# Sums of the norm for the seven products: from GpSimd and VectorE after one plain unit to VectorE alone after three

## The chip, the cores and the metric

The kernel runs on one core of a Trainium2 chip. The metric is the device time of one execution in microseconds, the median of several runs.

## What is computed

The reference is a two-layer backbone on 256 context and 512 latent tokens, 768 in all, of width 1024. Each layer has three mixers, a merge, and a gated MLP. The change touches the MLP of the first layer alone, the only one that runs over all 768 tokens:

```python
def conv_ffn(xn, w_up, conv_w, w_down):
    u = dwconv(xn @ w_up, conv_w)          # w_up is 1024 x 5632, conv of width 3 over positions
    a, gt = jnp.split(u, 2, axis=-1)
    return (a * jax.nn.silu(gt)) @ w_down  # w_down is 2816 x 1024
```

Here `xn` is the modulated norm of the residual stream.

## The kernel before

**Two parts of each number.** Each float32 operand of a product is split into a rounded high part and a low rest (`split`, line 220: a ScalarE copy makes the high part, a subtraction on VectorE the low one). A product is then three matmuls: high by high, high by low, low by high. The norm is held so too, as `n01xh` and `n01xl`, with eight k-blocks of 128 channels by 768 tokens.

**The MLP, `ffn` (line 1794).** The 22 column blocks of gates and of values run in pairs, `p0` = 0 and 2 inside groups `f0` = 0, 4, 8 and so on. For each pair first the gates (two blocks of 128 columns), then the values. One such pair of blocks is called a unit here: `f0g00` is the gates of pair 0, `f0a00` its values, `f0g02` and `f0a02` those of the second pair, `f0g40` the gates of the first pair of the next group. After `f0g40` stands the down projection `f0d0` of the group before it. A finished block goes through the convolution on VectorE (lines 1813 and 1815), the values through a product on GpSimd (line 1830), and then a split into `f0gh` and `f0gl` (lines 1831 and 1832).

**Two ways to compute a unit.** A plain unit (`gemm_fm`, line 247) takes each block with 8 k-blocks, three matmuls each, over 512 and then 256 tokens. A unit of seven products (`gemm7`, line 308) works on quarters, halves of k by halves of the tokens (384), and needs sums of quarters: four halves of weights made on GpSimd (`half`, lines 323 to 326) and four sums of the norm. It has seven groups of 12 matmuls on 384 tokens in place of eight. The groups and what they read of the sums, in the order of the code: `x1` (none), `x6` (sum 3), `x7` (sum 2), `x5` (sum 1), `x1` again (none), `x7` again (sum 4), `x5` again (none).

**The sums, `norm_sums` (line 622).** Four additions on GpSimd restore the quarters of the norm from its parts (line 632), four subtractions on VectorE make the sums (line 635), and four splits make their parts. Sum 2 is written over the quarter of the norm that no product of `gemm7` reads, so it has to wait for the plain units that read it. In the kernel before, `norm_sums` stands behind unit `f0a00`, and `f0g02` is the first unit of seven products.

**What sets the order.** Inside the MLP a scheduler orders each engine's instructions ahead of time by its own estimate of when each is ready, and among the ready by priority: program order, shifted by `high(offset)`. A negative offset puts work behind. The order on an engine is then fixed. Buffers of a tag share a number of slots: `q6` (line 156) holds the quarters, the sums and the `f0gh`, `f0gl` pairs, `s4` holds the fourth sum of weights. Weights come by DMA into four `wraw` slots and their parts into three `wh` and three `wl` slots. Between units, single products of the conditioning (`adp`, `adc`, lines 541 and 573) are put in.

Of the kernel before, what the change touches and what calls it, by code (L numbers as in the profile page):

```python
# [9 lines left out]
F32 = mybir.dt.float32  # L10
F32R = mybir.dt.float32r
I32 = mybir.dt.int32
AF = mybir.ActivationFunctionType
ALU = mybir.AluOpType
# [6 lines left out]
NT = SEQ + CTX  # L21
# [84 lines left out]
class Kernel:  # L106
# [113 lines left out]
    def split(self, h, l, x, eng=None):  # L220

        if eng is None:
            eng = self.nc.vector
        self.nc.scalar.copy(h, x)
        eng.tensor_tensor(out=l, in0=x, in1=h.bitcast(F32), op=ALU.subtract)  # L225
# [82 lines left out]
    def gemm7(self, src, c0, x, nt, done, nm):  # L308


        nc = self.nc
        n = nt // 2
        xh, xl, T = x
        r0, r1 = [self.wraw(src[:, c0 + 128 * b:c0 + 128 * b + 128], KD, 128, f"{nm}r{b}") for b in range(2)]
        s23 = self.pi.tile([128, KD, 128], F32, name=f"{nm}s23", tag="s23", bufs=2)
        s4 = self.pi.tile([128, 4, 128], F32, name=f"{nm}s4", tag="s4", bufs=2)
        lo, hi = slice(0, 4), slice(4, 8)

        def half(out, a, b, op):
            with self.high(self.prio):  # L320
                nc.gpsimd.tensor_tensor(out=out, in0=a, in1=b, op=op)

        half(s23[:, hi], r0[:, lo], r1[:, lo], ALU.subtract)
        half(r1[:, lo], r1[:, lo], r1[:, hi], ALU.add)
        half(s23[:, lo], r1[:, lo], r0[:, lo], ALU.subtract)
        half(s4, r0[:, hi], s23[:, lo], ALU.subtract)
        w0 = self.wsplit(r0, KD, 128, f"{nm}w0")
        w23 = self.wsplit(s23, KD, 128, f"{nm}w23")
        w1 = self.wsplit(r1, KD, 128, f"{nm}w1")
        w4 = self.wsplit(s4, 4, 128, f"{nm}w4", nc.gpsimd)  # L330

        def prod(ps, w, o, h, l, start, stop):

            mm = lambda a, b, **kw: nc.tensor.matmul(ps, a, b, skip_group_check=True, **kw)
            for k in range(4):
                mm(w[0][:, o + k, :], h(k), start=(start and k == 0), stop=False)
                mm(w[0][:, o + k, :], l(k), start=False, stop=False)
                mm(w[1][:, o + k, :], h(k), start=False, stop=(stop and k == 3))

        def of(k0, c):  # L340
            return [lambda k, v=v: v[:, k0 + k, c] for v in (xh, xl)]

        def oft(i):
            return [lambda k, v=v: v[:, k, :] for v in T[i]]
        t0, t1 = slice(0, n), slice(n, nt)
        x1, x7 = self.pl(f"{nm}x1")[:, 0:n], self.pl(f"{nm}x7")[:, 0:n]
        x6, x5 = self.pb(f"{nm}x6")[:, 0:n], self.pb(f"{nm}x5")[:, 0:n]
        c = [self.st(f"{nm}c{b}") for b in range(2)]
        u = self.st(f"{nm}u")
        p1, u2, u3 = u[:, 0:n], u[:, n:2 * n], c[1][:, 0:n]  # L350
        add = dict(op=ALU.add)
        prod(x1, w0, 0, *of(0, t0), True, True)
        nc.scalar.copy(p1, x1)
        prod(x6, w23, 0, *oft(3), True, True)
        nc.vector.tensor_tensor(out=u2, in0=x6, in1=p1, **add)
        prod(x7, w23, 4, *oft(2), True, True)
        nc.vector.tensor_tensor(out=u3, in0=x7, in1=u2, **add)
        prod(x5, w1, 0, *oft(1), True, True)
        nc.vector.tensor_tensor(out=c[1][:, t1], in0=x5, in1=u3, **add)
        prod(x1, w0, 4, *of(4, t0), False, True)  # L360
        nc.scalar.copy(c[0][:, t0], x1)
        prod(x7, w1, 4, *oft(4), False, True)
        nc.vector.tensor_tensor(out=c[1][:, t0], in0=x7, in1=u2, **add)
        prod(x5, w4, 0, *of(4, t1), False, True)
        nc.vector.tensor_tensor(out=c[0][:, t1], in0=x5, in1=u2, **add)
        for b in range(2):
            done(b, [(c[b][:, a:e], (a, e)) for a, e in ((0, SEQ), (SEQ, nt)) if e > a])
            self.ada_next()
# [253 lines left out]
    def norm_sums(self):  # L622


        nc, N = self.nc, self.N
        nm, n = N["nm"], N["nt"] // 2
        xh, xl = N["x"]
        q = lambda v, k, t: v[:, 4 * k:4 * k + 4, n * t:n * t + n]
        R = {}
        for k, t in ((0, 0), (0, 1), (1, 1), (1, 0)):  # L630
            R[k, t] = self.q6(f"{nm}R{k}{t}").rearrange("p (k t) -> p k t", k=4)
            nc.gpsimd.tensor_tensor(out=R[k, t], in0=q(xh, k, t).bitcast(F32), in1=q(xl, k, t).bitcast(F32), op=ALU.add)

        def sub(o, a, b):
            nc.vector.tensor_tensor(out=R[o], in0=R[a], in1=R[b], op=ALU.subtract)
        sub((0, 0), (0, 1), (0, 0))
        sub((0, 1), (1, 1), (0, 1))
        sub((1, 1), (1, 1), (0, 0))
        sub((1, 0), (1, 0), (1, 1))
        T = {}  # L640
        for i, o in ((3, (1, 1)), (1, (0, 0)), (4, (1, 0)), (2, (0, 1))):
            if i == 2:
                T[i] = q(xh, 0, 1), q(xl, 0, 1)
            else:
                T[i] = [self.q6(f"{nm}T{v}{i}", F32R).rearrange("p (k t) -> p k t", k=4) for v in "hl"]
            self.split(*T[i], R[o])
        return xh, xl, T

    def norm_sq(self, j, a, b, eng=None):
        nc, N = self.nc, self.N  # L650
# [1143 lines left out]
    def ffn(self, l, xs, nt):  # L1794
        nc = self.nc
        nm = f"f{l}"
# [4 lines left out]
        for f0 in range(0, NFF, FG):  # L1801
            fn = min(FG, NFF - f0)
            gh, gl = [], []
            for p0 in range(0, fn, 2):
                keep = {}

                def conv(ch, res, tag):
                    w = [self.V("fv", 132 * l + 44 * k + ch) for k in range(3)]
                    a = self.st(f"{nm}{tag}")
                    for ps, (s, e) in res:  # L1810
                        n = e - s
                        nc.scalar.activation(a[:, s:e], ps, AF.Copy, scale=w[1])
                        nc.vector.scalar_tensor_tensor(out=a[:, s + 1:e], in0=ps[:, 0:n - 1], scalar=w[0],
                                                       in1=a[:, s + 1:e], op0=ALU.mult, op1=ALU.add)
                        nc.vector.scalar_tensor_tensor(out=a[:, s:e - 1], in0=ps[:, 1:n], scalar=w[2],  # L1815
                                                       in1=a[:, s:e - 1], op0=ALU.mult, op1=ALU.add)
                    return a

                def done_g(b, ps):
                    a = conv(NFF + f0 + p0 + b, ps, f"g{f0}{p0}{b}")  # L1820
                    nc.scalar.activation(a[:, :nt], a[:, :nt], AF.Silu)  # L1821
                    keep[b] = a

                def done_a(b, ps):
                    a = conv(f0 + p0 + b, ps, f"a{f0}{p0}{b}")
                    if b == 0:
                        gh.extend(self.pairs(f"{nm}gh{f0}{p0}", 1, F32R))
                        gl.extend(self.pairs(f"{nm}gl{f0}{p0}", 1, F32R))
                    h = gh[-1][:, b, :nt]
                    nc.gpsimd.tensor_tensor(out=a[:, :nt], in0=a[:, :nt], in1=keep[b][:, :nt], op=ALU.mult)  # L1830
                    nc.scalar.copy(h, a[:, :nt])  # L1831
                    nc.vector.tensor_tensor(out=gl[-1][:, b, :nt], in0=a[:, :nt], in1=h.bitcast(F32), op=ALU.subtract)  # L1832

                if f0 + p0 == 0:
                    self.gemm_first(KD, xs, done_g, f"{nm}g{f0}{p0}")
                    x7 = None
                elif x7:
                    self.gemm7(U, D_FF + 128 * (f0 + p0), x7, nt, done_g, f"{nm}g{f0}{p0}")
                else:
                    self.gemm_fm(U, D_FF + 128 * (f0 + p0), 256, KD, xs, done_g, f"{nm}g{f0}{p0}")  # L1840
                if down and f0 + FG < NFF:
                    self.gemm_fm(*down)
                    down = None
                if x7:
                    self.gemm7(U, 128 * (f0 + p0), x7, nt, done_a, f"{nm}a{f0}{p0}")
                else:
                    self.gemm_fm(U, 128 * (f0 + p0), 256, KD, xs, done_a, f"{nm}a{f0}{p0}")
                    if f0 + p0 == 0 and nt == NT:
                        x7 = self.norm_sums()
            segs = [((a, b), Blocks(gh, a, b), Blocks(gl, a, b)) for a, b in segb]  # L1850

            def done_d(j, res):
# [8 lines left out]
        last = l == DEPTH - 1  # L1861
# [64 lines left out]
    def body(self):  # L1926
        nc, tc = self.nc, self.tc
# [4 lines left out]
        for l in range(DEPTH):  # L1932
            nt = NT if l < DEPTH - 1 else SEQ
# [8 lines left out]
            with tc.tile_pool(name=f"t{l + 1}", bufs=1, reuse_waits="tile") as self.ph:  # L1942
# [7 lines left out]
                else:  # L1950
                    self.ada_fill(2)
                self.spare = nt < NT
                with self.inner(f"u{l}", 10):
                    xs = self.ffn(l, xs, nt)
                self.dump_h(f"hf{l}", nt)
                if l + 1 < DEPTH:
# [81 lines left out]
```

## Time and profile before

| what | value |
|---|---|
| median of 3 runs | 2674.77 us (2668.91 to 2679.19) |
| the profiled execution | 2679.46 us, its span 2677.7 us |
| TensorE busy, share of the span | 97% |
| VectorE, ScalarE, GpSimd | 63%, 39%, 17% |
| TensorE's granted clock, mean | 0.987 of full |

The span is the time from the first to the last instruction. A matmul's duration holds its passage through the array, so the pace of a run of matmuls is read from the distance of their starts. DVE is VectorE, ACT is ScalarE, POOL is GpSimd, PE is TensorE, SP is the engine that issues the DMAs.

### The profile page before, as it was taken

How to read it: one execution, taken by the hardware profiler on the slowest of the kernel's cores; microseconds unless marked ns; L12 is line 12 of the kernel's file. 1: busy time of each engine (PE TensorE's matmuls, PEld its weight loads, DVE VectorE, ACT ScalarE, POOL GpSimd, SP SyncE). 2: the span in 40 equal slices, each digit the busy share in tenths (PEclk: the TensorE clock that was granted, in tenths of full speed). 3: DMA queues.
4: the chain of work that ended last, by engine and by line, in shares of the span. 5: the costliest groups of instructions: out<-in, count | busy, mean ns of one | idle time of the engine just before them, and what ended most of it. 6: DMA issues, size and time to landing. Idle time of an engine off the chain costs nothing.

```text
span 2677.7 us, 44644 instructions
## 1 busy us (share of the span) xinstructions
PE 2584.4 (97%) x17161; PEld 2234.9 (83%) x17161; DVE 1699.3 (63%) x3605; ACT 1047.1 (39%) x2313; POOL 463.1 (17%) x362
## 2 busy tenths in 40 slices
PE   7999999999999997999999999999999999999999
PEld 5987988888888886899999988888877878888887
DVE  6666566746534658676786777856676646655555
ACT  5433355333432234343443454344633333433332
POOL 1010000001110426154445320000000203100000
PEclk9999999999999998999999999999999999999999
DMA  8364343546746322322212243522367675333332
GB/s 284 94 178 134 90 121 88 151 137 195 214 160 230 120 87 87 107 83 79 71 54 81 87 141 102 154 71 77 114 193 219 184 249 150 91 94 95 95 103 75
DMA packets 485223, 344.19 MB, mean 129 GB/s; under 512 B 48168, under 2 KB 450322, under 8 KB 484242
## 3 DMA queue, kind: packets, MB, share of 16 engines
q1 hardware_dynamic: 484721, 338.19, 42.6%
q8 instruction: 135, 2.21, 0.3%
q10 hardware_dynamic: 288, 3.15, 0.3%
q14 instruction: 79, 0.64, 0.1%
HBM read 285.23 MB, written 56.03 MB: 127 GB/s over the span
## 4 chain that ended last, share of the span: by engine, by line
PE 75%; DVE 10%; DMA 9%; issue 2%; ACT 1%; POOL 1%; SPq 1%; DVEq 0%; POOLq 0%; ACTq 0%
PE mg04p L265 1%; PE mg04p L266 1%; PE mg04p L264 1%; PE y0p L265 1%; PE y0p L264 1%; PE y0p L266 1%; PE adp L541 1%; PE mg14p L264 1%; PE mg14p L265 1%; PE mg14p L266 1%; PE y1p L264 1%; DMA m1mb<-g1rd 1%; PE y0op L264 1%; PE y0op L266 1%; PE y0op L265 1%
## 5 line engine op out<-in xcount | busy, mean ns | idle before, releaser
L1830 POOL TENSOR_TENSOR f1a<-f1a,f1g 128x512 f32<-128x512 f32 x22 | 28.5, 1295 | 311.8 <-DVE f1a L1815 292.3
L541 PE MATMUL adp<-ad,s 128*32 128x256 f32 x640 | 55.7, 405 | 6.5 <-DMA ad<-ada_w 5.6
L1830 POOL TENSOR_TENSOR f0a<-f0a,f0g 128x768 f32<-128x768 f32 x22 | 51.9, 2360 | 57.8 <-DVE f0a L1815 53.4
L1752 POOL TENSOR_TENSOR y0a<-y0a,y0g 128x768 f32<-128x768 f32 x16 | 33.2, 2079 | 118.1 <-DVE y0g L1749 115.8
L1107 POOL TENSOR_TENSOR m0qz<-m0qz,m0e 64x512 f32<-64x512 f32 x12 | 15.5, 1295 | 165.5 <-DVE mg04s5l L225 68.7
L541 PEld LDWEIGHTS adp<-ad,s 128*32 128x32 f32 x640 | 18.5, 112 | 26.3 <-issue 14.2
L1832 DVE TENSOR_TENSOR f0gl<-f0a,f0gh 128x768 fp32r<-128x768 f32 x22 | 31.0, 1411 | 8.5 <-ACT f0gh L1831 8.5
L1752 POOL TENSOR_TENSOR y1a<-y1a,y1g 128x512 f32<-128x512 f32 x16 | 24.2, 1513 | 57.8 <-DVE y1g L1749 56.6
L544 ACT COPY adr<-adp 128x256 f32<-128x256 f32 x40 | 14.8, 370 | 44.0 <-PE adp L541 42.8
L1831 ACT CAST f0gh<-f0a 128x768 fp32r<-128x768 f32 x22 | 18.4, 838 | 33.5 <-POOL f0a L1830 33.5
L1013 ACT ACTIVATE mg0t<-mg04p 128x512 f32<-128x512 f32 (+1 forms) x40 | 19.5, 486 | 25.2 <-PE mg04p L266 20.7
L1107 POOL TENSOR_TENSOR m1qz<-m1qz,m1e 64x512 f32<-64x512 f32 x8 | 11.2, 1406 | 102.9 <-DMA m1mb<-g1rd 45.7
L1821 ACT ACTIVATE f0g<-f0g 128x768 f32<-128x768 f32 x22 | 18.5, 846 | 22.8 <-DVE f0g L1815 22.8
L1749 DVE SCALAR_TENSOR_TENSOR y0g<-y0g,y0p 128x512 f32<-128x512 f32 (+1 forms) x32 | 17.3, 549 | 15.8 <-PE y0p L266 14.0
L1821 ACT ACTIVATE f1g<-f1g 128x512 f32<-128x512 f32 x22 | 13.9, 630 | 32.5 <-DVE f1g L1815 32.5
L1096 DVE SCALAR_TENSOR_TENSOR m0mb<-m0mb,g0a,cst 128x128 f32<-128x128 f32 x48 | 16.6, 404 | 15.3 <-DMA m0mb<-g0rd 14.3
L1773 DVE SCALAR_TENSOR_TENSOR hr<-y0op,y0gh,hr 128x512 f32<-128x512 f32 (+1 forms) x16 | 9.9, 617 | 25.8 <-PE y0op L266 25.8
L1169 POOL TENSOR_TENSOR rt<-rc,rw 128x256 f32<-128x256 f32 x4 | 3.0, 745 | 115.7 <-PE b0pk L1239 54.8
L1832 DVE TENSOR_TENSOR f1gl<-f1a,f1gh 128x512 fp32r<-128x512 f32 x22 | 15.1, 685 | 10.9 <-ACT f1gh L1831 10.7
L1831 ACT CAST f1gh<-f1a 128x512 fp32r<-128x512 f32 x22 | 13.5, 616 | 16.6 <-POOL f1a L1830 16.6
L1729 DVE TENSOR_TENSOR y0l<-y0ld,y0h 128x768 fp32r<-128x768 f32 x12 | 12.8, 1091 | 11.3 <-ACT y0h L1728 11.3
L1098 ACT ACTIVATE m0mb<-m0mb 128x512 f32<-128x512 f32 x12 | 7.6, 631 | 30.1 <-DVE m0mb L1096 25.4
(4586 smaller groups left out, 10220.2 us busy)
## 6 DMA issues: line engine op xcount, KB each, us to landing
ad<-ada_w SPq DMA_DIRECT2D x96, 512.0 KB, 4.3
mg04r<-w_in SPq DMA_DIRECT2D x20, 512.0 KB, 5.1
mg14r<-w_in SPq DMA_DIRECT2D x20, 512.0 KB, 6.0
y0g<-mg SPq DMA_DIRECT2D x24, 384.0 KB, 4.4
mg<-mg0t SPq DMA_DIRECT2D x24, 256.0 KB, 3.1
y0r<-w_branch SPq DMA_DIRECT2D x12, 512.0 KB, 3.6
mg<-mg1t SPq DMA_DIRECT2D x24, 256.0 KB, 3.5
y1r<-w_branch SPq DMA_DIRECT2D x12, 512.0 KB, 3.9
```

The lines of the kernel that those rows point to most:

```text
L264: nc.tensor.matmul(o, hv[:, k, :], xh[:, k, :], start=(k == 0), stop=False)
L265: nc.tensor.matmul(o, hv[:, k, :], xl[:, k, :], start=False, stop=False)
L266: nc.tensor.matmul(o, lv[:, k, :], xh[:, k, :], start=False, stop=(k == nk - 1))
L541: nc.tensor.matmul(ps[32 * j:32 * j + 32, 0:256], self.s32[:, 2 * k:2 * k + 32], raw[:, j, :], start=(q == 0), stop=(q == 1), tile_positio ...
L1013: nc.scalar.activation(s, o, AF.Tanh, scale=0.5)
L1107: nc.gpsimd.tensor_tensor(out=qd[r, d], in0=qd[r, d], in1=e2[r], op=ALU.mult)
L1749: nc.vector.scalar_tensor_tensor(out=(a if i == BR[0] else gt)[:, s:e], in0=gt[:, s:e], scalar=1.0, in1=ps, op0=ALU.add, op1=ALU.mult)
L1752: nc.gpsimd.tensor_tensor(out=a[:, :nt], in0=a[:, :nt], in1=gt[:, :nt], op=ALU.add)
L1821: nc.scalar.activation(a[:, :nt], a[:, :nt], AF.Silu)
L1830: nc.gpsimd.tensor_tensor(out=a[:, :nt], in0=a[:, :nt], in1=keep[b][:, :nt], op=ALU.mult)
L1831: nc.scalar.copy(h, a[:, :nt])
L1832: nc.vector.tensor_tensor(out=gl[-1][:, b, :nt], in0=a[:, :nt], in1=h.bitcast(F32), op=ALU.subtract)
```

## The change

The sums are taken from the two parts by VectorE alone: for sums 1 and 2 three instructions each (subtract the high parts, subtract the low parts, add), for sums 3 and 4 two each, with a split behind each sum. The call moves from behind `f0a00` to between `f0g02` and `f0a02`, with priority 3000 behind. The second pair is now plain too, and `f0g40` is the first unit of seven products. The split of sum 2 is issued on its own behind `f0a02`, at the usual priority. The `q6` slots in the MLP go from 10 to 11, those of `s4` from 2 to 1.

```diff
-        s4 = self.pi.tile([128, 4, 128], F32, name=f"{nm}s4", tag="s4", bufs=2)
+        s4 = self.pi.tile([128, 4, 128], F32, name=f"{nm}s4", tag="s4", bufs=1)
...
-        R = {}
-        for k, t in ((0, 0), (0, 1), (1, 1), (1, 0)):
-            R[k, t] = self.q6(f"{nm}R{k}{t}").rearrange("p (k t) -> p k t", k=4)
-            nc.gpsimd.tensor_tensor(out=R[k, t], in0=q(xh, k, t).bitcast(F32), in1=q(xl, k, t).bitcast(F32), op=ALU.add)
...
+        def diff(i, j, k):
+
+            for o, v in zip(R, (xh, xl)):
+                op(o, q(v, *j).bitcast(F32), q(v, *k).bitcast(F32), ALU.subtract)
+            op(R[0], R[0], R[1], ALU.add)
+
+        def less(o, j, a):
+            op(o, q(xh, *j).bitcast(F32), a, ALU.subtract)
+            op(o, o, q(xl, *j).bitcast(F32), ALU.add)
...
+        diff(1, (0, 1), (0, 0))
+        split(1, R[0])
+        less(R[1], (1, 1), R[0])
+        split(3, R[1])
+        less(R[0], (1, 0), R[1])
+        split(4, R[0])
+        diff(2, (1, 1), (0, 1))
+        T[2] = q(xh, 0, 1), q(xl, 0, 1)
+
+        def last():
+            self.split(*T[2], R[0])
+        return (xh, xl, T), last
...
+                if f0 + p0 == 2 and nt == NT:
+                    with self.high(-3000):
+                        sums, last_sum = self.norm_sums()
                 if x7:
                     self.gemm7(U, 128 * (f0 + p0), x7, nt, done_a, f"{nm}a{f0}{p0}")
                 else:
                     self.gemm_fm(U, 128 * (f0 + p0), 256, KD, xs, done_a, f"{nm}a{f0}{p0}")
-                    if f0 + p0 == 0 and nt == NT:
-                        x7 = self.norm_sums()
+                    if f0 + p0 == 2 and nt == NT:
+                        x7 = sums
+                        last_sum()
...
-                with self.inner(f"u{l}", 10):
+                with self.inner(f"u{l}", 11):
```

## Rows read from the trace of the kernel before

**Rows 1.** The page: busy time by engine, and TensorE in 40 slices.
```profile
PE 2584.4 (97%) x17161; PEld 2234.9 (83%) x17161; DVE 1699.3 (63%) x3605; ACT 1047.1 (39%) x2313; POOL 463.1 (17%) x362
...
PE   7999999999999997999999999999999999999999
```
**Rows 2.** Stages: busy us (and instructions) of each engine, clock, DMA share, GB/s.
```profile
1040.10:1053.50 13.40, 2.87 (x19) 0.72 (x18) 11.46 (x6) 2.18 (x3) 13.40 (x4) 0.63 0.66 195
1053.50:1073.20 19.70, 12.00 (x38) 9.86 (x38) 19.70 (x10) 6.48 (x6) 19.70 (x9) 0.65 0.00 0
```
**Rows 3.** The chain that ended last, in order of time: start, us, what.
```profile
1033.40 8.58 POOL n01R L632 x2
...
1042.01 4.95 DVE n01R L635
...
1052.03 3.20 DVE n01R L635
```
**Rows 4.** TensorE in order of time: start, us, instruction, [idle before <-releaser].
```profile
1018.94 0.39 PE L264 MATMUL f0a00p<-n01xh,f0a00s0h 128*128 128x512 f32 x1
...
1024.54 0.39 PE L264 MATMUL f0a00p<-n01xh,f0a00s1h 128*128 128x512 f32 x1
...
1031.33 0.28 PE L264 MATMUL f0a00p<-n01xh,f0a00s1h 128*128 128x256 f32 x1
...
1034.15 0.34 PE L334 MATMUL f0g02x<-n01xh,f0g02w0h 128*128 128x384 f32 x1
...
1036.23 0.38 PE L573 MATMUL adc<-cst,adr 128*128 128x128 f32 x2
1036.55 1.07 PE L541 MATMUL adp<-ad,s 128*32 128x256 f32 x16
...
1094.89 0.34 PE L334 MATMUL f0g40x<-n01xh,f0g40w0h 128*128 128x384 f32 x1
```
**Rows 5.** VectorE in order of time: sums, splits and convolutions.
```profile
1020.25 1.22 DVE L225 TENSOR_TENSOR f0a00s1l<-f0a00r,f0a00s1h 128x1024 fp32r<-128x1024 f32 x1
...
1032.18 2.04 DVE L1832 TENSOR_TENSOR f0gl<-f0a,f0gh 128x768 fp32r<-128x768 f32 x1
1034.14 0.74 DVE L1813 SCALAR_TENSOR_TENSOR f0a<-f0a00p,vec,f0a 128x511 f32<-128x511 f32 x1
...
1038.59 0.47 DVE L1813 SCALAR_TENSOR_TENSOR f0a<-f0a00p,vec,f0a 128x255 f32<-128x255 f32 x1
...
1050.21 1.74 DVE L635 TENSOR_TENSOR n01R<-n01R,n01R 128x1536 f32<-128x1536 f32 x1
...
1060.67 2.84 DVE L225 TENSOR_TENSOR n01Tl<-n01R,n01Th 128x1536 fp32r<-128x1536 f32 x1
```
**Rows 6.** GpSimd in order of time: the additions, a product, the fourth weight sums.
```profile
1029.32 1.85 POOL L1830 TENSOR_TENSOR f0a<-f0a,f0g 128x768 f32<-128x768 f32 x1
...
1033.37 16.88 POOL L632 TENSOR_TENSOR n01R<-n01xh,n01xl 128x1536 f32<-128x1536 f32 x4
1050.21 3.41 POOL L1830 TENSOR_TENSOR f0a<-f0a,f0g 128x768 f32<-128x768 f32 x1
...
1161.76 1.31 POOL L225 TENSOR_TENSOR f0a40w4l<-f0a40s,f0a40w4h 128x512 fp32r<-128x512 f32 x1
...
1177.16 2.03 POOL L225 TENSOR_TENSOR f0g42w4l<-f0g42s,f0g42w4h 128x512 fp32r<-128x512 f32 x1
```
**Rows 7.** ScalarE: the copy of one sum, with its wait.
```profile
1055.27 1.47 ACT L224 CAST n01Th<-n01R 128x1536 fp32r<-128x1536 f32 x1 [1.81 <-DVE n01R L635]
```
**Rows 8.** Stages as in rows 2: one plain unit here, then plain gates earlier.
```profile
1015.00:1034.00 19.00, 19.00 (x124) 15.98 (x123) 11.40 (x15) 9.44 (x13) 8.51 (x6) 1.00 0.27 84
...
830.00:880.00 50.00, 50.00 (x290) 44.01 (x290) 28.46 (x37) 11.59 (x13) 8.47 (x5) 1.00 0.63 207
```
**Rows 9.** TensorE by line, 1034 to 1095 us: busy, mean ns, idle before.
```profile
L541 PE MATMUL adp<-ad,s 128*32 128x256 f32 x48 | 4.5, 469 | 5.6 <-DMA ad<-ada_w 5.6
...
L573 PE MATMUL adc<-cst,adr 128*128 128x128 f32 x6 | 1.4, 329 | 0.5 <-ACT adr L544 0.5
```

More of the change, by code (lines that the diff above doesn't have):

```diff
@@ L628, in norm_sums, with op, split @@
         q = lambda v, k, t: v[:, 4 * k:4 * k + 4, n * t:n * t + n]
-        R = {}
-        for k, t in ((0, 0), (0, 1), (1, 1), (1, 0)):
-            R[k, t] = self.q6(f"{nm}R{k}{t}").rearrange("p (k t) -> p k t", k=4)
-            nc.gpsimd.tensor_tensor(out=R[k, t], in0=q(xh, k, t).bitcast(F32), in1=q(xl, k, t).bitcast(F32), op=ALU.add)
[L634 to L639, printed above, removed]
-        T = {}
[L641 to L647, printed above, removed]
+        R = [self.q6(f"{nm}R{i}").rearrange("p (k t) -> p k t", k=4) for i in range(2)]
+        T = {}
+        def op(o, a, b, op):
+            nc.vector.tensor_tensor(out=o, in0=a, in1=b, op=op)
+        def diff(i, j, k):
[5 more added lines that the diff above has]
+            op(o, o, q(xl, *j).bitcast(F32), ALU.add)
+        def split(i, v):
+            T[i] = [self.q6(f"{nm}T{p}{i}", F32R).rearrange("p (k t) -> p k t", k=4) for p in "hl"]
+            self.split(*T[i], v)
+        diff(1, (0, 1), (0, 0))
[9 more added lines that the diff above has]
+        return (xh, xl, T), last
     def norm_sq(self, j, a, b, eng=None):
```

## The prediction

> **What bounds the kernel now.** I read the busy shares first: TensorE is busy for 97% of the span, and of the 40 slices only the first and the sixteenth fall below nine tenths [rows 1]. The sixteenth holds the start of the first layer's MLP, so I cut that into stages [rows 2]. From 1040.1 us, 6 us into the first unit of seven products, TensorE is busy for 2.87 of 13.40 us, and then for 12.00 of 19.70 us at a mean clock of 0.65, a mix of its two levels of 1.2 and 2.4 GHz, after an idle stretch. GpSimd is busy all the while, and VectorE nearly so. The chain of waits says why: it runs through the additions on GpSimd into the subtractions on VectorE, and these into the splits [rows 3]. TensorE waits for the sums of the norm.
>
> **How much is lost there.** The first matmul of `f0g40` starts at 1094.89 us, so 60.74 us go by from the first one of `f0g02` [rows 4]. The work in them: one group of twelve matmuls on 384 tokens takes 2.08 us (1034.15 to 1036.23), so two units of seven groups take 29.1 us [rows 4]. Beside them ran 48 small products of the conditioning and six transposes [rows 9]; 16 of the first took 1.07 us at full clock and two of the second 0.32 (1036.23 to 1036.55), 4.2 us in all [rows 4]. That is 33.3 us of work; 27.4 us were lost, to waiting and to the lower clock together.
>
> **The change, part by part.** *The plain pair.* A plain block is 24 matmuls on 512 tokens (1018.94 to 1024.54, 5.60 us) and 24 on 256 (1031.33 to 1034.15, 2.82 us), 8.42 us [rows 4]. The four blocks of `f0g02` and `f0a02` then take 33.7 us where the two units of seven products take 29.1: 4.6 us are added, all on TensorE's path. If nothing of the wait were left, `f0g40` would start 33.7 + 4.2 = 37.9 us after the end of `f0a00`, at 1072 us, and the gain would be 60.7 - 37.9 = 22.8 us.
>
> *Do plain units keep TensorE full?* In `f0a00` it has no gap over 19 us, and in the mixers' plain gates, with the same conditioning between them, none over 50 us [rows 8]. So I put the feeding of the plain pair at nothing; its cover is the weights' splits and loads running one block (8.42 us) ahead.
>
> *The sums on VectorE.* GpSimd loses four additions that took 16.88 us [rows 6]. VectorE had eight instructions of 128x1536 and now has fourteen: ten for the sums, four in the splits. One such instruction took 1.74 us at its shortest and 2.84 us in the splits beside a busy GpSimd [rows 5]. Fourteen are 24.4 us by the one and 39.8 by the other. I take 1.74, since GpSimd has only the products of line 1830 (1.85 us, four of them) and the halves of the weights left in the plain stretch, and I keep 2.84 for the range. The copies on ScalarE, 1.47 us each [rows 7], stay four; ScalarE is busy for half of the plain stretch [rows 8], so only the last one is on the path.
>
> *Is there room?* The first additions of the kernel before began at 1033.37, just behind the first `f0gl` [rows 5, 6]; both ask for slots of `q6`, and the new sums ask behind `f0gl` too, so I let them begin there. Until 1072 that is 38 us. VectorE's own work in it: a block's convolution is 2.4 us (0.74 + 0.75 + 0.47 + 0.48, two of these shown), its weights 1.22, a `f0gl` up to 2.04 [rows 5]. The last block of `f0a00` (4.5), three blocks of the pair and the weights of the fourth (about 14), and two splits of weights for `f0g40` (2.4) make 21 us; 17 are free. Thirteen instructions, without the last split, ask for 22.6 us. So sums 1, 3 and 4 (ten, 17.4 us) are just made when `f0g40` starts, and the three for sum 2 are 5.6 us late. Behind them stand the ScalarE copy (1.47) and the last split (1.74), and between them what VectorE owes the fourth block (about 5 us). Sum 2 is there some 9 to 14 us into `f0g40`. Two groups of 2.08 us lie ahead of its first reader in the code, four if the order made ahead puts `x5` and the second `x1` before it: 4.2 to 8.3 us of cover. The stall is 1 to 10 us; I take 5.5.
>
> *The wait that is added.* The last split's copy waits on ScalarE for the last matmul of `f0a02` that reads the overwritten quarter; behind it on ScalarE stand casts of weights for `f0g40`, wanted 6 us later, and so at most its 1.47 us are passed on. The sums issue no DMA, so no queue of SP moves.
>
> *A slot less of `s4`.* The fourth sum of weights of a unit now waits until the unit before has split its own. In steady work that split ends at 1163.1 and the next one starts at 1177.2 [rows 6]: 14 us for 1.3 us of work. I cost it at nothing; without that cover it would be those 1.3 us in each of 18 units, 23 us in all. One slot more of `q6` takes no wait away that the rows show, and adds none: nothing.
>
> **The same by the Trainium skill.** The first subtraction lasted 4.95 us, of which it lay behind an addition for some 3.2 us and ran for 1.74; the product on GpSimd that began with a VectorE instruction of 1.74 us took 3.41 us in place of 1.85 [rows 5, 6, 3]. The Trainium skill, page "SBUF — State Buffer", section "Who interferes with whom", says that a VectorE instruction with two SBUF inputs and a GpSimd instruction that reads SBUF exclude each other for the whole of the first. By that rule, which the trace agrees with, the two engines did not share the sums before: four additions of at least some 3.2 us and eight of 1.74 make about 27 us in a row, fourteen make 24.4, so the change of engine alone would be worth 2 or 3 us and the place behind the plain units would be the rest. The sum above goes by the place already.
>
> **Sum.** 22.8 us less a stall of 5.5 is 17.3 us off the profiled 2679.46 us, 0.65%. That execution lies 0.18% above the median; carried over to the median of 2674.77 it gives 2657 us.
>
> **Rivals.** (a) *No stall is left.* If the sums may begin in the gaps of `f0a00` already, where 7.6 of 19 us are free [rows 8], the room is 24 us and all thirteen fit. Then the gain is 22.8 us, 2652. For it: nothing they read is still being written there, and only the slots hold them back. Against it: the additions before did not start so early.
>
> (b) *VectorE is held up by GpSimd.* If each sum meets a product or a half of the weights, at 2.84 us, thirteen take 36.9 us in the place of 22.6, and the stall grows by 14 to some 10 to 23 us. The gain is 0 to 13, with 6 in the middle, 2669. For it: 3.20 and 2.84 us were the rule beside GpSimd [rows 3, 5]. Against it: GpSimd has no more than 18 us of work in these 38. By that page of the Trainium skill this is the case in which each of the fourteen waits for a whole GpSimd instruction of 1.3 to 1.85 us.
>
> (c) *Slower: the sums are put behind too far.* Priority 3000 behind could leave all of them until `f0a02` is done. Then 39.8 us at the long duration and two copies of 1.47 stand behind 1072, less 8.3 us of cover: a stall of 34, with some 5 us for the lower clock behind it, an estimate from the 0.65 that followed the idle time [rows 2]. Against the 23 gained this is 16 us slower, 2691. At 1.74 us each it would stay at the old time; it is slower only if the whole chain starts after about 1065. Against it: VectorE has 40% free in a plain unit, and nothing ready but the sums to fill it.
>
> (d) *The wait was not the sums alone.* For 5.6 us of the idle time the conditioning's products waited for their weights [rows 9]. If these or a plain block's weights come late in the new order too, 5 to 12 us of the gain go: 2667.
>
> **How the numbers follow.** Chances: the forecast 0.42, (a) 0.25, (b) 0.20, (c) 0.06, (d) 0.07. The likeliest gives 2657. The range runs from just beyond (a), with 6 us for what a new order of the later stages may bring or take, to just beyond the middle of (b): 2646 to 2672. About 0.5% (13 us) is what a measurement of this kernel can tell from no change. Faster by more: (a), most of the forecast, little of (b), 0.66; within: most of (b), (d), a part of the forecast, 0.27; slower: (c) and a bad order later, 0.07.
>
> **What would show it.** In the profile after: no gap on TensorE from 1034 to about 1072; `f0g40` starting near 1072 and waiting for sum 2 by some 5 us; fourteen VectorE instructions of 128x1536 near 1.74 us; no addition of 16.88 us on GpSimd; a clock of 1.00 through the plain pair. It is wrong if the sums' instructions start only behind 1065, if TensorE idles inside the plain pair, or if later stages are longer than before.

## The result and the profile after

The kernel after took 2662.76 us (median of 9 runs, 2657.27 to 2669.48) against 2677.04 us for the kernel before beside it (9 runs): a ratio of 0.9945, 95% interval 0.9931 to 0.9960. That is 0.55% faster by the ratio, and 14.3 us between the medians; the forecast was 17.3 us. The profiled execution has a span of 2662.2 us, 15.5 us under the 2677.7 us of the one before.

The page of the kernel after, its busy row and TensorE's 40 slices, answers [rows 1]:

```profile
PE 2583.1 (97%) x17185; PEld 2235.5 (84%) x17185; DVE 1692.6 (64%) x3599; ACT 1042.1 (39%) x2305; POOL 422.7 (16%) x348
...
PE   7999999999999999999999999999999999999999
```

The 7 in the sixteenth slice is gone, and so are 40 us of GpSimd's busy time: 17 of them are the four additions, the rest the halves of weights, mainly of the two units that are plain now. The shares hardly moved: TensorE is at 97% of a shorter span. The stage that held the loss, kernel after, answers [rows 2] (each engine's busy us and instructions, clock, DMA share, GB/s):

```profile
1040.00:1050.00 10.00, 10.00 (x68) 8.17 (x67) 10.00 (x11) 2.69 (x4) 3.10 (x1) 1.00 0.57 158
1050.00:1060.00 10.00, 10.00 (x59) 8.71 (x58) 10.00 (x11) 5.91 (x7) 0.13 (x1) 1.00 0.18 53
1060.00:1072.00 12.00, 10.97 (x77) 8.95 (x76) 10.87 (x12) 5.00 (x7) 9.21 (x4) 1.00 0.06 16
```

TensorE is full but for 1.0 us and VectorE but for 1.1, at a clock of 1.00, where [rows 2] had TensorE at 2.87 of 13.40 us. TensorE in order of time, kernel after, answers [rows 4]:

```profile
1035.54 0.39 PE L264 MATMUL f0g02p<-n01xh,f0g02s0h 128*128 128x512 f32 x1
...
1053.80 0.39 PE L264 MATMUL f0a02p<-n01xh,f0a02s0h 128*128 128x512 f32 x1
...
1065.63 0.47 PE L264 MATMUL f0a02p<-n01xh,f0a02s1h 128*128 128x512 f32 x1 [1.02 <-DVE f0g L1827]
...
1074.04 0.42 PE L334 MATMUL f0g40x<-n01xh,f0g40w0h 128*128 128x384 f32 x1 [0.64 <-DVE ada L580]
...
1080.81 0.34 PE L334 MATMUL f0g40x<-n01xl,f0g40w23h 128*128 128x384 f32 x1
```

`f0g40` starts at 1074.04 us, 38.50 us behind the first matmul of `f0g02`; before, it was 60.74 us. The only waits on the way are 1.02 us for a convolution of `f0g` on VectorE, in the middle of `f0a02`, and 0.64 us ahead of `f0g40`. The chain of waits of the kernel after, answering [rows 3] (start, us, what):

```profile
1071.57 1.66 DVE n01R L633
1073.23 0.66 DVE f0a L1827
1074.04 4.42 PE f0g40x L334 x24
```

A sum on VectorE is still on the chain, but it delays the start by under 1 us where [rows 3] showed 8.58 and 4.95 us of one addition pair and one subtraction. VectorE in order of time, kernel after, answering [rows 5]:

```profile
1034.76 1.23 DVE L225 TENSOR_TENSOR f0g02s1l<-f0g02r,f0g02s1h 128x1024 fp32r<-128x1024 f32 x1 [6.38 <-ACT f0g02s1h L224]
1035.90 0.95 DVE L1844 TENSOR_TENSOR f0gl<-f0a,f0gh 128x768 fp32r<-128x768 f32 x1
1036.77 1.75 DVE L633 TENSOR_TENSOR n01R<-n01xh 128x1536 f32<-128x1536 f32 x1
...
1049.00 2.74 DVE L633 TENSOR_TENSOR n01R<-n01R,n01xl 128x1536 f32<-128x1536 f32 x1
...
1062.38 2.44 DVE L633 TENSOR_TENSOR n01R<-n01xl 128x1536 f32<-128x1536 f32 x1
...
1071.49 1.74 DVE L633 TENSOR_TENSOR n01R<-n01xh 128x1536 f32<-128x1536 f32 x1
...
1077.63 1.76 DVE L225 TENSOR_TENSOR n01xl<-n01R,n01xh 128x1536 fp32r<-128x1536 f32 x1
```

The first sum stands right behind the first `f0gl`, after an idle time of 6.38 us one instruction earlier. Twelve of the fourteen instructions are done before `f0g40` begins; the last one, the low part of sum 2, ends at 1079.4, 5.3 us into it. The first matmul that reads it stands at 1080.81 in TensorE's list, so no matmul of `f0g40` waited for it. GpSimd and ScalarE in order of time, kernel after, answering [rows 6, 7]:

```profile
1028.52 1.84 POOL L1842 TENSOR_TENSOR f0a<-f0a,f0g 128x768 f32<-128x768 f32 x1 [29.84 <-DVE f0a L1827]
1046.90 3.23 POOL L1842 TENSOR_TENSOR f0a<-f0a,f0g 128x768 f32<-128x768 f32 x1 [16.54 <-DVE f0a L1827]
...
1076.12 1.48 ACT L224 CAST n01xh<-n01R 128x1536 fp32r<-128x1536 f32 x1 [3.93 <-DVE n01R L633]
```

**Where the 15.5 us went.** From the first matmul of `f0a00` to that of `f0d0` the two profiled executions took 102.4 and 80.2 us: 22.2 us gained. Given back: 1.4 us ahead of `f0a00`, where every engine has the same order in both kernels; 1.2 us from `f0d0` to the end of that MLP, with ten small products of the conditioning (0.7 us by [rows 4]) that moved there from the stage; 3.3 us in the second layer ahead of its MLP (first matmul of `c10k` to that of `y1t`); 0.8 us behind it. Within the 1.2 us stands a wait that the kernel before did not have:

```profile
1454.79 0.44 PE L334 MATMUL f0a162x<-n01xh,f0a162w4l 128*128 128x384 f32 x1 [2.11 <-POOL f0a162w4l L225]
```

That is the fourth sum of weights, whose `s4` has one slot now.

### The profile page after: what moved, and what is told of

It reads as the page before. It is cut to its first block, busy times and chain, and to the rows that moved or that the text cites. A ratio compares the mean times of both kernels' runs of the same rounds, so it can differ in the third digit from the quotient of the medians.

```text
span 2662.2 us, 44654 instructions
## 1 busy us (share of the span) xinstructions
PE 2583.1 (97%) x17185; PEld 2235.5 (84%) x17185; DVE 1692.6 (64%) x3599; ACT 1042.1 (39%) x2305; POOL 422.7 (16%) x348
## 4 chain that ended last, share of the span: by engine, by line
PE 79%; DVE 9%; DMA 7%; issue 2%; ACT 1%; POOL 1%; SPq 1%; DVEq 0%; ACTq 0%; POOLq 0%
PE mg04p L265 2%; PE mg04p L264 2%; PE mg04p L266 2%; PE y0p L265 1%; PE adp L541 1%; PE y0p L264 1%; PE y0p L266 1%; DMA m0mb<-g0rd 1%; PE y1p L264 1%; PE y1p L266 1%; PE y1p L265 1%; PE mg14p L264 1%; PE mg14p L265 1%; PE mg14p L266 1%; PE y0op L266 1%
## 5 line engine op out<-in xcount | busy, mean ns | idle before, releaser
L1761 DVE SCALAR_TENSOR_TENSOR y0g<-y0g,y0p 128x512 f32<-128x512 f32 (+1 forms) x32 | 17.3, 549 | 16.0 <-PE y0p L266 14.0
L1833 ACT ACTIVATE f1g<-f1g 128x512 f32<-128x512 f32 x22 | 13.9, 630 | 32.5 <-DVE f1g L1827 32.5
L1844 DVE TENSOR_TENSOR f1gl<-f1a,f1gh 128x512 fp32r<-128x512 f32 x22 | 15.1, 685 | 10.9 <-ACT f1gh L1843 10.8
```

Source lines behind the costliest of these rows:

```text
L1761: nc.vector.scalar_tensor_tensor(out=(a if i == BR[0] else gt)[:, s:e], in0=gt[:, s:e], scalar=1.0, in1=ps, op0=ALU.add, op1=ALU.mult)
```

## The experiments

All runs in one table: the ratio to the kernel before, the two stretches of the MLP, and the second layer ahead of its MLP, in us of one profiled execution each.

| kernel | ratio [95%] | `f0a00` to `f0d0` | `f0d0` to `f0tp` | `c10k` to `y1t` |
|---|---|---|---|---|
| before | 1 | 102.4 | 426.2 | 707.6 |
| after | 0.9945 [0.9931, 0.9960] | 80.2 | 427.4 | 710.9 |
| after, once more | 0.9953 [0.9937, 0.9969] | 79.3 | 428.1 | 714.3 |
| old engines, new place | 0.9947 [0.9931, 0.9963] | 82.8 | 433.9 | 704.8 |
| new engine, old place | 1.0025 [1.0013, 1.0036] | 108.5 | 427.1 | 709.6 |
| before with the new slots | 1.0009 [0.9998, 1.0020] | 102.5 | 428.6 | 710.6 |
| after with the old slots | 0.9933 [0.9920, 0.9946] | 78.3 | 426.9 | 715.8 |
| eight more instructions | 0.9973 [0.9961, 0.9985] | 91.1 | 430.0 | 710.7 |
| sums asked for earlier | 0.9909 [0.9895, 0.9922] | 78.8 | 429.3 | 705.8 |
| earlier, no plain group | 0.9986 [0.9975, 0.9997] | 97.9 | 427.1 | 705.6 |
| earlier, old engines, `f0a02` of seven | 0.9960 [0.9947, 0.9973] | 82.4 | 428.4 | 717.1 |
| earlier, `f0a02` of seven | 0.9882 [0.9865, 0.9899] | 80.6 | 426.5 | 700.7 |
| the last with the old slots | 0.9890 [0.9878, 0.9903] | 80.2 | 425.9 | 700.0 |

### The kernel after once more

No edit: this shows how far two executions of one program differ.

> The changed kernel once more, to see which parts of its profile repeat. The first profile had f0g40 start 20.9 us earlier than before (1074.0 against 1094.9) though its stage before the change began 1.3 us later, and only 15.5 us of that were left at the end: about 4.6 us were given back in the second layer between 1960 and 2176 us, where the order of the instructions differs little. Theory A (the giving back is the spread of single executions): time near 2663, f0g40 again some 79 to 80 us behind the start of f0g00 (before: 101.6), and the second layer's stages shifted by another amount than in the first profile. Theory B (the new order in the second layer costs 4 to 5 us every time): the stretch from the first mg14 matmul to the first y1 matmul is again about 241 us, where the kernel before has 236.

The stage came out at 79.3 us (80.2), `f0g40` again starting without a wait for the sums. But from `c10k` to `b1a0pq` it took 139.7 us in place of 134.5, and from `mg14` to `y1` 237.6 in place of 240.8. The same program differs by 3 to 5 us in such a stretch, so a difference of that size in one pair of traces says nothing by itself. The gain of the stage is far above it.

### The place alone

```
-                    if f0 + p0 == 0 and nt == NT:
-                        x7 = self.norm_sums()
+                    if f0 + p0 == 2 and nt == NT:
+                        x7 = sums
+                        last_sum()
```

The additions stay on GpSimd and the subtractions on VectorE; the call, the held-back split and the slots are those of the change.

> The place alone: four additions on GpSimd and four subtractions on VectorE as before, but called between f0g02 and f0a02, with the second pair plain, the split of sum 2 behind it, 11 q6 slots and one s4 slot. Theory of the place: the additions run from about 1035 to 1052 beside plain units that keep TensorE full, the sums are there by about 1070, f0g40 starts within 3 us of 1074, and the time is 2660 to 2667, 10 to 17 us faster than before. Rival, the engine: what helped is that VectorE no longer waits for GpSimd's additions; then most of the gain is gone, 2670 to 2678, with f0g40 starting behind 1080 or waiting inside for its sums by 5 us or more.

```profile
1030.33 16.59 POOL L632 TENSOR_TENSOR n01R<-n01xh,n01xl 128x1536 f32<-128x1536 f32 x4
...
1067.19 0.47 PE L264 MATMUL f0a02p<-n01xh,f0a02s1h 128*128 128x512 f32 x1 [3.58 <-DVE f0g L1819]
```

GpSimd's four additions (first line, GpSimd in order) take the same time as in [rows 6], and the stage is 82.8 us: 19.6 of the 22.2 us are there without any change of engine. TensorE (second line) waits once, 3.58 us, for a convolution. So the place, with its plain pair, makes the gain of the stage; the engine is worth some 2.6 us of it here, where two executions of the change itself differ by 0.9. That the ratio is that of the change is luck: the rest of the MLP takes 6.5 us more (433.9 against 427.4), with waits for the fourth sums of weights of 2.1, 1.7 and 1.5 us among them, and the second layer 6.1 us less.

### The engine alone

The old call behind `f0a00`, `f0g02` of seven products, with the sums on VectorE as in the change:

```
-                        x7 = self.norm_sums()
+                        x7, last_sum = self.norm_sums()
+                        last_sum()
```

> The engine alone: the sums made on VectorE from the two parts as in the changed kernel, but called behind f0a00, with f0g02 the first unit of seven products, as before (slots as in the changed kernel). Theory of the place: the chain of 14 instructions of 1.74 to 2.84 us begins near 1036 and TensorE waits for it with nothing else to do; f0g40 starts at 1085 to 1097 (before: 1094.9) and the time is 2667 to 2680, at most 10 us faster and most likely 2 to 3, the difference of the time that the two engines hold each other up. Rival, the engine: 10 us or more faster, 2667 or less, f0g40 before 1085.

TensorE in order of time, then VectorE instructions of the sums, then the two stretches as in [rows 2]:

```profile
1056.40 0.69 PE L334 MATMUL f0g02x<-n01Th,f0g02w23h 128*128 128x384 f32 x1 [6.61 <-ACT n01Th L224]
...
1075.07 0.69 PE L334 MATMUL f0g02x<-n01xh,f0g02w23h 128*128 128x384 f32 x1 [9.14 <-ACT n01xh L224]
```

```profile
1062.21 2.83 DVE L633 TENSOR_TENSOR n01R<-n01R,n01xl 128x1536 f32<-128x1536 f32 x1
...
1075.05 1.76 DVE L225 TENSOR_TENSOR n01xl<-n01R,n01xh 128x1536 fp32r<-128x1536 f32 x1 [1.54 <-ACT n01xh L224]
```

```profile
1040.00:1056.00 16.00, 5.41 (x36) 3.01 (x32) 16.00 (x15) 4.79 (x6) 11.30 (x6) 0.66 0.55 165
1056.00:1075.00 19.00, 8.12 (x24) 7.29 (x24) 17.45 (x9) 3.27 (x3) 10.10 (x4) 0.59 0.00 0
```

It is slower than the kernel before, by 0.25% and 6.1 us of the stage. The prediction's side sum (four additions and eight instructions "in a row", 27 us, against fourteen, 24.4 us) had the wrong sign for the old place. The rows show two things that it left out. GpSimd turns to the halves of the weights instead, 21.4 us in these 35, and beside them six of the fourteen instructions took 2.8 us or more and not 1.75; VectorE is busy for 33.45 of the 35 us. And the new code makes the sums one behind the other, sum 2 last. In the kernel before, the low part of sum 2 was the first of the four to be made, by VectorE's list:

```profile
1055.16 2.82 DVE L225 TENSOR_TENSOR n01xl<-n01R,n01xh 128x1536 fp32r<-128x1536 f32 x1
```

Here it begins at 1075.05, and TensorE's longest wait, 9.14 us, is for sum 2. So this edit changes the order of the sums together with the engine. How much of the 6.1 us is which was not tested: no run has the new engine with the old order.

### The slots alone

```
-        s4 = ... tag="s4", bufs=2)
+        s4 = ... tag="s4", bufs=1)
...
-                with self.inner(f"u{l}", 10):
+                with self.inner(f"u{l}", 11):
```

This is the edit of the kernel before alone; the converse, two slots and ten in the kernel after, ran too.

> The kernel before with only the two sizes of the change: one slot of s4 in place of two and 11 of q6 in place of 10. The fourth sum of weights then waits on GpSimd for the split of the unit before. Theory (no cost, since 14 us lie between the two splits in steady work): within 3 us of before, and units of seven products still 14.9 us long. Rival (the wait shows in each unit): 10 to 23 us slower, units longer by up to 1.3 us.

> The changed kernel with two slots of s4 and 10 of q6, the sizes of the kernel before. In the changed kernel and in the kernel before with the two new sizes alone TensorE waits 2.1 to 2.2 us for GpSimd's w4l in unit f0a162, in the kernel before not. Theory (one slot of s4 makes that wait): it is gone, and the stage from f0g40 to f0tp is 444 us as before, not 445.3 to 446. With 10 slots the second f0gl has to wait for a sum's slot; that is on no path of TensorE, so f0g40 starts within 2 us of the changed kernel's 61.5 to 62.3 us behind f0a00, and the time is 1 to 2 us less. Rival: the slot of q6 is needed, f0g40 3 us or more later.

With one slot, TensorE waits in this kernel too, in the same unit:

```profile
1475.85 0.44 PE L334 MATMUL f0a162x<-n01xh,f0a162w4l 128*128 128x384 f32 x1 [2.21 <-POOL f0a162w4l L225]
```

With two slots the wait in the kernel after is gone; in its place stands one of 1.8 us for `f0a162c` on VectorE, which the kernel before has as well. So the slot's price is about 1 us here (2.1 and 0.7 us of waits against 1.8), in one of the 18 units. The waits were longer elsewhere: in the traces of the ten executions with one slot TensorE's waits for the fourth sums of weights come to 2.0 to 5.4 us, in one to three units, and in the three with two slots to 0 to 0.6 us. Timed, neither kernel differs from its neighbour by more than the intervals allow. The eleventh slot of `q6` shows no use here.

### Eight instructions more on VectorE

Eight of the ten instructions of the sums are made twice, with the same results: 13.9 us more for VectorE at 1.74 us each.

```
+                for _ in range(2):
                     op(o, q(v, *j).bitcast(F32), q(v, *k).bitcast(F32), ALU.subtract)
             op(R[0], R[0], R[1], ALU.add)
+            op(R[1], R[0], R[1], ALU.add)
...
+            for _ in range(2):
                 op(o, q(xh, *j).bitcast(F32), a, ALU.subtract)
```

> The changed kernel with eight of the sums' VectorE instructions made twice (18 in place of 10, 13.9 us more at 1.74 us each; the results are the same). It measures how much room VectorE has left in the plain pair. Theory of my sum (17 us of room for 22.6 us, the rest under the cover of f0g40's first groups): no room is left, so most of the 13.9 us shows, f0g40 or its groups start 8 to 14 us later and the time is 2671 to 2680, near the kernel before. Rival (TensorE has other work to take, and the sums have slack): 4 us or less.

TensorE's waits from 1076 to 1107 us (us in total, times, longest), the larger ones:

```profile
PE adp L541 <- DMA ad<-ada_w: 5.0, 2, 3.6
PE adc L573 <- DVE ada L574: 2.3, 1, 2.3
PE f0g40x L334 <- ACT f0g40u L353: 1.5, 1, 1.5
PE f0g40x L334 <- ACT n01xh L224: 1.0, 1, 1.0
PE f0g40x L334 <- DVE n01xl L225: 0.8, 1, 0.8
```

The plain pair is untouched (`f0a00` to `f0g40` 60.6 us), and the whole price is paid inside `f0g40`: 30.5 us to `f0d0` instead of 17.9, with the clock at 0.54 in its last 15 us. The stage is 10.9 us longer for 13.9 us of work, and half the gain is lost. Its end is not the same work in both: 30 small products more stand in it (2 us by [rows 4]), and 24 matmuls of `f0g40` stand behind it. So the room that the prediction counted was nearly used up; how many us were left can't be read from this. Of the waits listed only 1.8 us are for sum 2; most are for other work: the conditioning's weights, its reduction on VectorE, and a copy on ScalarE. That these came late because of the added work is likely, since nothing else was edited, but the chain from one to the other was not followed.

### The sums asked for earlier

The call of `norm_sums` moves ahead of `f0a00`, and nothing else changes:

```
-                if f0 + p0 == 2 and nt == NT:
+                if f0 + p0 == 0 and nt == NT:
                     with self.high(-3000):
                         sums, last_sum = self.norm_sums()
```

> The changed kernel with the call of the sums ahead of f0a00 in place of behind f0g02 (still 3000 behind in priority; the second pair plain, f0g40 the first unit of seven products). Theory of the slots: the sums ask for their q6 slots ahead of the first f0gh and f0gl, so they begin in the gaps that VectorE has in f0a00, near 1017 in place of 1036, and are done some 15 us earlier. Then the wait of about 1 us inside f0a02 and the 0.9 us ahead of f0g40 go: f0g40 starts 60 to 61 us behind f0a00 (changed kernel: 62.3 and 61.5 in two profiles), the time is up to 2 us less than the changed kernel's, ratio to before 0.993 to 0.996. Rival (the start is set by something else, the norm itself or the order): the first sum again near 1036 and nothing moved.

VectorE in order of time, and the stretch of [rows 8]:

```profile
1012.21 1.75 DVE L633 TENSOR_TENSOR n01R<-n01xh 128x1536 f32<-128x1536 f32 x1
```

```profile
1015.00:1034.00 19.00, 18.40 (x117) 15.19 (x116) 19.00 (x23) 10.47 (x13) 0.00 (x0) 1.00 0.23 70
```

The first sum begins at 1012.2 instead of 1036.8 us, before the norm is complete, and VectorE fills all 19 us where it had 11.40 before. What held the sums back was the place of the call, and not the data; the offset of 3000 is the same in both. That the place acts through the slots of `q6`, handed out in the order of the calls, is an argument: no run separates the slots from the program order, and a late call with ten slots in place of eleven began its sums no later (0.7 us ahead of the first matmul of `f0g02`; the change began level with it and 1.2 us behind). The stage gains 1.4 us at most by it (78.8 us, against 80.2 and 79.3 in the change and 78.3 in the change with the old slots): little was left to gain, and TensorE has no wait above 0.6 us there. The ratio of 0.9909 lies outside the stated 0.993 to 0.996. It is some 8 us lower than the stage explains, and most of these lie in the second layer (705.8 against 710.9 and 714.3 us).

### Earlier, and no plain group

The same early call with `f0g02` of seven products at once:

```
-                    if f0 + p0 == 2 and nt == NT:
+                    if f0 + p0 == 0 and nt == NT:
                         x7 = sums
                         last_sum()
```

> The sums on VectorE asked for ahead of f0a00 (as in the kernel with the early call), but no plain group behind it: f0g02 is the first unit of seven products again, 4.6 us less of plain work. If the plain group is needed as cover (theory): the sums begin near 1012 us, VectorE cannot have them before about 1055, TensorE waits 13 to 18 us in f0g02, and from the first matmul of f0a00 to that of f0d0 it takes 88 to 98 us instead of 78.8; ratio 0.995 to 1.000. Rival, that the early start alone is what counts and the plain group only adds its 4.6 us: at most 84 us for the stage and a ratio of 0.989 to 0.992.

TensorE in order of time:

```profile
1060.75 0.69 PE L334 MATMUL f0g02x<-n01xh,f0g02w23h 128*128 128x384 f32 x1 [9.70 <-ACT n01xh L224]
...
1063.30 0.69 PE L334 MATMUL f0g02x<-n01xl,f0g02w23h 128*128 128x384 f32 x1 [1.86 <-DVE n01xl L225]
```

97.9 us: the theory's case. With the sums on VectorE and no plain pair, the earlier start is worth 10.6 us of the stage (108.5 with the late call); against the kernel before, with its other engines, 4.5 are left. The pair is worth 19 more, its 4.6 us of extra work paid. TensorE has sum 2, the last one made, only at 1063.3 us, and the one long wait is for it; whether another order of the sums would shorten it was not tested. VectorE and GpSimd are both nearly full until then (21.62 and 20.86 of 24.40 us from 1036.3 to 1060.7).

### Earlier, with `f0a02` of seven products

Early sums, and the seven products begin one unit sooner, at `f0a02`; then the same with the old slots; then with the old mix of engines.

```
+                if f0 + p0 == 2 and nt == NT:
+                    x7 = sums
+                    last_sum()
                 if x7:
                     self.gemm7(U, 128 * (f0 + p0), x7, nt, done_a, f"{nm}a{f0}{p0}")
```

> As the early call, and f0a02 is already a unit of seven products, so one plain unit less (2.3 us of TensorE's work saved). By the count of VectorE's room: from 1017 to 1053 some 16 to 18 us are free for 24.4 us of sums, so the last of them are 7 to 9 us late, less 4 to 8 us of cover: TensorE waits 0 to 5 us in f0a02 and the time is within 3 us of the changed kernel's, 2661 to 2668. Theory of the full group (the sums need both plain units): a wait of 8 us or more, and 4 us or more slower than the changed kernel.

> The fastest kernel so far (sums on VectorE asked for ahead of f0a00, f0a02 the first unit of seven products) with two slots of s4 and ten of q6 again. If the single slot costs only the one wait of about 2 us at f0a162, the stage from f0d0 to the second layer is 1 to 2 us shorter than 426.5 us without that wait, and the ratio lies between 0.986 and 0.989 (that kernel: 0.9882). Rival, that the tenth and eleventh slot of q6 mattered for the early start: the sums begin later than 1012 us, TensorE waits in f0a02, and the ratio is above 0.990.

> The old mix of engines (four additions on GpSimd, eight instructions of 128x1536 on VectorE) at the best place found: asked for ahead of f0a00, where GpSimd is idle and the slots of q6 are free, with f0a02 the first unit of seven products. That engines matter little if the place is good: the additions begin near 1012 us at 3.2 to 4 us each and are done near 1030, VectorE owes 13.9 us instead of 24.4, all sums are ready before 1050, TensorE does not wait, and from the first matmul of f0a00 to that of f0d0 it takes 78 to 80 us as in the early VectorE kernels (78.8 and 80.6); ratio to before 0.987 to 0.992. Rival, that the two engines in a row are the slow part wherever they stand: a wait of over 3 us is left at f0a02, as in the kernel with the old mix behind the plain unit (82.8 us for the stage), and the ratio is 0.993 to 0.996.

The first two are the fastest kernels here, 0.9882 and 0.9890, about 0.6% under the change. The first of them was expected within 3 us of the change and is some 17 us under it. Its sums were in time, with 0.34 us of waiting at most in `f0a02`, so one plain unit less is cover enough for an early call. Yet the stage did not shorten by the 2.3 us of plain work that are saved (80.6 and 80.2 us, 78.8 with the early call alone). Work of the conditioning moved in: 84 of its small products and transposes in twelve groups stand in the stage and not 70 in eight, and from the start of each group to the next matmul of the MLP they take 8.7 us together and not 6.0. The gain in time lies in the second layer, 700.7 and 700.0 us. TensorE's waits there, from 1680 to 2285 us, first in the kernel after:

```profile
PE b1a3pp L1336 <- ACT b1a3P L1329: 4.2, 1, 4.2
PE y1p L264 <- DVE y1a L1761: 3.1, 1, 3.1
PE c11vp L1547 <- DVE c11r L1543: 2.7, 1, 2.7
PE m1pt L1161 <- DVE m1hs L1155: 2.7, 1, 2.7
```

and in the kernel with `f0a02` of seven products:

```profile
PE b1a3pp L1336 <- ACT b1a3P L1329: 2.6, 2, 2.1
...
PE y1p L264 <- DVE y1g L1761: 0.5, 1, 0.5
```

The waits at `c11vp` and `m1pt` are gone, and that at `y1p` is 0.5 us. None of these is for the sums. Most of the programs have an order of their own in the second layer, and the traces let the order be held against the time. The change, both times, and the change with the old slots have one and the same order on all four engines between the first matmuls of `c10k` and `y1t`: 710.9, 714.3 and 715.8 us. The two fastest kernels share another: 700.7 and 700.0 us. So one order differs by up to 5 us between executions, and these two orders by 10 to 16; that difference goes with the program. Which edit brings a good order was not found.

The old mix of engines at the early place waits at none of the seven products, as the theory had it, but the stage is 82.4 us. GpSimd, then VectorE, then TensorE's waits:

```profile
1021.46 8.50 POOL L632 TENSOR_TENSOR n01R<-n01xh,n01xl 128x1536 f32<-128x1536 f32 x2 [2.86 <-DVE n01xl L737]
```

```profile
1022.62 3.98 DVE L635 TENSOR_TENSOR n01R<-n01R,n01R 128x1536 f32<-128x1536 f32 x1
...
1027.43 3.62 DVE L225 TENSOR_TENSOR f0a00s1l<-f0a00r,f0a00s1h 128x1024 fp32r<-128x1024 f32 x1
```

```profile
PE f0g02p L264 <- DVE f0a L1819: 2.0, 2, 1.1
PE f0g00p L296 <- DVE n01xl L737: 1.4, 1, 1.4
PE f0a00p L266 <- DVE f0a00s1l L225: 1.1, 1, 1.1
```

Beside the additions a subtraction on VectorE took 3.98 us (1.74 alone) and a split of weights 3.62 (1.2 elsewhere), and TensorE waits 4.5 us in the plain units, for the split, the norm and the convolutions. Neither of the two stated cases: the sums were in time, and their neighbours were late. And 16.4 of the 20.4 us between its span and that of the fastest kernel lie in the second layer again (717.1 against 700.7 us).

## Why the prediction was right, and where it was not

**What bounds the kernel: right.** The sums were what TensorE waited for. Taken off its path they gave 22.2 us, the 4.6 us of plain work paid, of the 22.8 that were the most by the forecast.

**The plain pair: right.** From `f0g02` to `f0g40` it took 38.50 us; forecast 37.9, with all of the conditioning's small products inside, of which sixteen fell into `f0g40` instead. Feeding it, forecast at nothing, cost the 1.02 us wait. Without the pair the gain of the stage is 4.5 us instead of 23.6 (both with the early call).

**When the sums may begin: right.** They began behind the first `f0gl`, at 1036.8 (forecast about 1033; `f0a00` itself ran 1.4 us later here). That an earlier call would use the gaps of `f0a00` was rival (a)'s argument; the early call showed it. That it is the slots that hold the sums back was not shown: with the old engines at the new place the first addition began at 1030.33 us, and the first `f0gl` at 1034.84.

**VectorE's room: mis-sized.** Forecast 17 us beside 21 us of its own work, so ten instructions by the start of `f0g40`. Twelve were done. From 1036.77 to 1074.04 VectorE was idle for 1.14 us, and its own work there was 16.0 us by the sum of its durations and not 21: one `f0gl` at 0.94 us where the forecast had two at up to 2.04, four splits of weights and not six.

**The stall of 5.5 us: wrong.** It was none. Sum 2 was ready 5.3 us into `f0g40` (forecast 9 to 14), inside the cover of 6.8 us: two groups of matmuls and, by the order made ahead, sixteen products of the conditioning that moved into the unit. The cover is within the forecast's 4.2 to 8.3; what was wrong is when the sums were done, by the mis-sized room. In the stage this is rival (a)'s outcome, 22.2 us against its 22.8, but not by its cause: the sums did not begin in the gaps of `f0a00`.

**The duration of the sums' instructions: right.** Eleven of fourteen took 1.74 to 1.76 us, three took 2.16, 2.44 and 2.74 beside GpSimd; 26.6 us in all between the two bounds of 24.4 and 39.8, near the lower one. Rival (b) did not come, since GpSimd has little work until 1060. Its price was also mis-summed: a stall of 1 to 10 us that grows by 14 is 15 to 24 us and not 10 to 23, so the middle of its gain is 3 us and not 6, 2672.

**The slot of `s4`: missed.** Forecast at nothing by the steady cover of 14 us. One unit of the 18 lacks that cover, `f0a162`, and pays about 1 us here; in other kernels with one slot up to three units waited.

**The rest of the program: missed as a term.** 1.4, 1.2, 3.3 and 0.8 us were given back. They stood in the range only, as 6 us for a new order. That the total came out 3 us from the forecast is due to two errors against each other: 5.5 us of a stall that did not come, and some 7 us that were given back elsewhere. Of these the 1.4 us, and part of the 3.3, are no more than two executions of one program differ; the change's order of the second layer took 710.9 to 715.8 us in three executions, the kernel before 707.6 in one, so how much of the rest is order and how much is spread stays open.

**Priority 3000 behind, rival (c): did not come.** The sums started at 1036.77 us, not behind 1065. No run leaves the priority as it was, so what it does is not shown. **Rival (d):** no wait for weights or conditioning beyond 0.64 us in the plain stretch.

**By the Trainium skill,** page "SBUF — State Buffer", section "Who interferes with whom", the change of engine alone was put at 2 to 3 us. At the new place the two engine mixes differ by 2.6 us in the stage (82.8 and 80.2), a like amount; at the old place, for which it was worked out, the new engine loses 6.1 us, with sum 2 made last. The rows bear out the exclusion itself (3.98 us for a subtraction beside an addition, 1.74 alone; 3.23 us for a product on GpSimd that began beside a VectorE instruction of the sums, 1.84 alone).

## What to carry to other kernels

When a long preparation must precede a faster form of the work, run the plain form for as long as the preparation takes: 4.6 us of extra matmuls saved 19 us net here, and the choice of engine 2.6 at that place. Count the room on the preparing engine instruction by instruction over that very stretch. Ask what the place of the call lets start early: it moved the first sum by 24 us here, worth 10.6 us without the plain form and hardly anything with it. A gain in one stage is not the gain of the program: read the later stages for waits of their own before a difference of a few us is put down to the edit.

## What the runs showed of the hardware

A wait of TensorE cost more than its length, since the clock was low afterwards: in the early kernel without the plain group, matmuls of 128x384 behind the waits of 9.70 and 1.86 us took 0.52 us and began 0.32 us apart, where they take 0.34 and begin 0.17 apart at full clock (twelve in 2.08 us, [rows 4]). One of them, and the stretches:

```profile
1064.11 0.52 PE L334 MATMUL f0g02x<-n01xh,f0g02w23h 128*128 128x384 f32 x1
```

```profile
1036.30:1060.70 24.40, 11.89 (x76) 9.28 (x76) 21.62 (x20) 7.88 (x11) 20.86 (x10) 0.89 0.45 130
1060.70:1072.00 11.30, 8.74 (x25) 7.83 (x26) 4.76 (x4) 1.66 (x4) 3.60 (x2) 0.50 0.11 30
```

In the second one TensorE worked at 0.50, the 1.2 GHz level, for all of 11.3 us, although it was busy for 8.74 of them; in the kernel after, where no wait from 1040 to 1072 us exceeded 1.02 us, every stretch shown has 1.00.
